# Seven gate products placed last in the input part with a PSUM bank of their own, put-off closing sums, and low-rank weights by head pair

## The chip, the cores and the metric

The kernel runs on one core of a Trainium2 chip. The metric is the device time of one execution in microseconds; the lower the better. TensorE is PE in the rows (its weight loads are PEld), VectorE DVE, ScalarE ACT, GpSimd POOL and SyncE SP.

## The reference

One hybrid encoder layer is computed for a prompt of 1024 rows and a sample of 256 rows, in float32 with 1024 channels. Cut to the part that the change touches:

```python
h = rmsnorm(x, norm_mix) * (1.0 + sc1) + sh1          # sh, sc, g: silu(c) @ w_ada + b_ada
p = h @ w_in                                          # 672 | 1792 | 2048 columns
p_mla, p_rwkv, p_gate = ...
xs = pf + mu_shift * (centred_shift(pf) - pf)         # pf = p_rwkv; r, k, v, wd, ad, gd are parts of xs
g = sigmoid(gd) @ w_gate_up
kk = k * k_k / norm over the head;  tw = tanh(wd)
for d in range(2):                                    # two directions
    wlog = -softplus(-(w0[d] + tw @ w_decay_up[d])) - 0.5
    a = sigmoid(a0[d] + ad @ w_iclr_up[d])
    k_d = k * (1.0 + (a - 1.0) * k_a)
    y = y + wkv_scan(...);  bonus_k = bonus_k + k_d
out = (group_norm(y) * lnx_w + lnx_b + sum(r * bonus_k * r_k) * v) * g
gm, gr = split(sigmoid(p_gate))
x = x + g1 * ((gm * o_mla + gr * o_rwkv) @ w_out)     # then a SwiGLU FFN
```

## The kernel before, in words

Both sequences stand side by side as T = 1280 columns, with channels on the 128 partitions. A product of 1024 by 128 channels takes the columns in three chunks of 512, 512 and 256 (`CH`). To keep float32 precision each operand is split into a high and a low part, and `gemm` (line 67) does three matmuls for each of 8 row tiles and each chunk: 72 in all, into three PSUM banks at a time. `split_w` loads the weights (`wraw`, line 51), casts the high part on ScalarE (`whi`, line 53) and subtracts on GpSimd or VectorE (`wlo`, line 55).

After the normalised input `hh`, `hl` is there, the input part has 27 such products. First come two for the low-rank inputs. Then four head pairs follow (`pt`), each with products for k, r and v; each product is evacuated to `pp` (line 299, two buffers) and shifted on VectorE (lines 302 to 305). Per pair and direction four small low-rank products (line 352) go through two `aux` banks to tanh on ScalarE (lines 384 and 391), and VectorE makes `kd` and `ka` from them; results are spilled to DRAM. At the pair's end come `bk`, a head sum (line 363) and the bonus. Then `phase_mla_in` has six products with two norms and the rotary keys `kpe`, and after them the first seven of the sixteen gate products, whose tanh (line 457) is spilled. The other nine are computed much later. The pieces of the w_ada product that are needed later (lines 162, 170 to 182) are called by a hook inside the products: one piece after row tiles 1, 4 and 7, each with a load of 512 KB into one of two `araw` buffers; after four pieces the result is transposed by eight small products, and it takes an `araw` buffer for this (`am4`).

The order of the instructions on each engine is laid out when the kernel is built: a planner with a cost model gives the engine the ready instruction that was emitted first, so what is emitted later fills places that are free in the planner's own timeline. Buffers and banks are waited for one by one. On the chip every engine follows its list in order, and so do the DMA queues of SP, ACT and POOL. PSUM has eight banks: five for products (`mm`), two `aux`, one for the w_ada pieces. Attention follows; its tiles use the memory of `hh`, `hl` and of the weight buffers.

## Time and profile before

| | |
|---|---|
| time, 3 runs | 2739.36, 2742.91 (median), 2749.71 us |
| profiled execution | 2739.23 us, span 2737.5 us |
| TensorE busy | 2528.6 us (92%), 16458 matmuls |
| VectorE busy | 1464.8 us (54%) |
| ScalarE busy | 987.5 us (36%) |
| GpSimd busy | 844.4 us (31%) |
| DMA | 273.39 MB, mean 100 GB/s |

The busy time is that of one profiled execution, and the shares are of its span. In rows of a timeline the first number is the start in us from the span's start, the second the length; "x3" means three instructions merged into one row, and the bracket says how long the engine stood idle before and what ended that. In the rows by stretch, the numbers behind the length are the busy us of PE, PEld, DVE, ACT and POOL with the count of instructions, then the granted TensorE clock as a share of full speed, the share of DMA time and GB/s.

### The profile page before, as it was taken

The page shows a single profiled execution, that of the slowest core. Times are in us where ns is not written, and L with a number is a line of the kernel's source. Part 1 is how long each engine was busy: PE and PEld are TensorE (multiplying, and loading weights), DVE is VectorE, ACT ScalarE, POOL GpSimd, SP SyncE. Part 2 cuts the span into 40 slices and gives each one's busy share as a digit, 9 for nine tenths or more (in the row PEclk, how much of TensorE's full clock was granted, in tenths as well). Part 3 has the DMA queues.
Part 4 walks back from the last instruction along what each step waited for, and adds up shares of the span by engine and source line. Part 5 has one row for each costly group of instructions (what it writes and reads, how often), then busy time and mean ns, then how long its engine had stood idle before and what let it go on. Part 6 is the DMA issues. An engine that isn't in the chain of part 4 may idle for free.

```text
span 2737.5 us, 41260 instructions
## 1 busy us (share of the span) xinstructions
PE 2528.6 (92%) x16458; PEld 2139.5 (78%) x16458; DVE 1464.8 (54%) x2436; ACT 987.5 (36%) x1853; POOL 844.4 (31%) x820
## 2 busy tenths in 40 slices
PE   5998879999998889899989988899999999999997
PEld 3776558888987778888877767778888888888886
DVE  6664553237777688988986557362222222222228
ACT  4432223236776645556553233241110111101114
POOL 1112122121015654455544466342111111111123
PEclk9999889999999888899978899999999999999998
DMA  7645432210003432533445755221111111111113
GB/s 292 213 179 194 166 123 67 77 48 16 18 15 86 147 102 80 164 104 117 147 128 175 233 173 152 94 70 62 39 39 32 38 39 39 39 39 39 39 39 131
DMA packets 175279, 273.39 MB, mean 100 GB/s; under 512 B 14752, under 2 KB 103792, under 8 KB 175088
## 3 DMA queue, kind: packets, MB, share of 16 engines
q1 hardware_dynamic: 169328, 244.55, 27.9%
q0 software_dynamic: 5760, 26.22, 2.4%
q8 instruction: 129, 2.11, 0.3%
q14 instruction: 62, 0.51, 0.1%
HBM read 202.51 MB, written 68.20 MB: 99 GB/s over the span
## 4 chain that ended last, share of the span: by engine, by line
PE 71%; DVE 19%; DMA 3%; issue 3%; ACT 2%; POOL 2%; SPq 1%; POOLq 0%; DVEq 0%; ACTq 0%
PE mm L67 46%; PE fp L1004 7%; DVE W L832 3%; PE s L592 3%; DVE xt L830 3%; PE o L626 2%; PE proj L525 2%; PE t L613 2%; PE py L877 1%; DVE lt L772 1%; DVE tt L834 1%; PE ada_ps L170 1%; PE lora L352 1%; PE pA L785 1%; PE hsum L363 1%
## 5 line engine op out<-in xcount | busy, mean ns | idle before, releaser
L55 POOL TENSOR_TENSOR wlo<-wraw,whi 128x512 fp32r<-128x512 f32 (+2 forms) x226 | 404.0, 1789 | 1165.3 <-ACT whi L53 1129.1
L53 ACT CAST whi<-wraw 128x1024 fp32r<-128x1024 f32 (+2 forms) x241 | 193.9, 806 | 954.8 <-issue 466.8
L67 PE MATMUL mm<-h2h,whi 128*128 128x512 f32 (+1 forms) x1056 | 280.2, 358 | 1.5 <-ACT whi L53 1.5
L67 PE MATMUL mm<-h2h,wlo 128*128 128x512 f32 (+1 forms) x1056 | 279.8, 358 | 1.3 <-POOL wlo L55 1.3
L67 PE MATMUL mm<-h2l,whi 128*128 128x512 f32 (+1 forms) x1056 | 279.4, 357 | 0.0
L67 PE MATMUL mm<-g,whi 128*128 128x512 f32 (+1 forms) x1056 | 240.1, 359 | 6.2 <-DVE ft L1209 5.6
L1004 PE MATMUL fp<-x,whi 128*128 128x256 f32 (+1 forms) x912 | 220.5, 334 | 12.6 <-DVE gt L1139 4.1
L67 PEld LDWEIGHTS mm<-g,whi 128*128 128x128 f32 x1056 | 177.4, 189 | 38.0 <-issue 5.7
L67 PEld LDWEIGHTS mm<-h2h,whi 128*128 128x128 f32 x1056 | 177.5, 189 | 33.2 <-ACT whi L53 1.8
L67 PEld LDWEIGHTS mm<-h2h,wlo 128*128 128x128 f32 x1056 | 177.5, 189 | 32.9 <-POOL wlo L55 2.2
L67 PEld LDWEIGHTS mm<-h2l,whi 128*128 128x128 f32 x1056 | 177.4, 188 | 31.5 <-issue 0.5
L67 PE MATMUL mm<-hh,whi 128*128 128x512 f32 (+1 forms) x648 | 188.1, 368 | 11.0 <-ACT pp L299 6.3
L67 PE MATMUL mm<-hl,whi 128*128 128x512 f32 (+1 forms) x648 | 185.8, 364 | 7.0 <-DVE hl L244 7.0
L1221 DVE SCALAR_TENSOR_TENSOR x<-mm,g2h,x 128x512 f32<-128x512 f32 (+1 forms) x144 | 86.9, 656 | 195.9 <-PE mm L67 195.6
L1004 PEld LDWEIGHTS fp<-x,whi 128*128 128x128 f32 x912 | 165.9, 215 | 25.4 <-ACT whi L53 5.3
L67 PE MATMUL mm<-hh,wlo 128*128 128x512 f32 (+1 forms) x648 | 184.4, 364 | 0.0
L1209 DVE SCALAR_TENSOR_TENSOR ft<-ft,mm 128x512 f32<-128x512 f32 (+1 forms) x66 | 36.1, 593 | 223.5 <-ACT ft L1208 223.4
L1004 PE MATMUL fp<-x,wlo 128*128 128x256 f32 (+1 forms) x456 | 151.4, 333 | 0.4 <-POOL wlo L55 0.4
L1210 DVE TENSOR_TENSOR ft<-ft,mm 128x512 f32<-128x512 f32 (+1 forms) x66 | 36.0, 593 | 215.9 <-PE mm L67 215.9
L67 PEld LDWEIGHTS mm<-hh,whi 128*128 128x128 f32 x648 | 116.3, 193 | 38.5 <-ACT pp L299 8.0
L67 PEld LDWEIGHTS mm<-hl,whi 128*128 128x128 f32 x648 | 116.6, 192 | 30.6 <-DVE hl L244 8.2
L67 PE MATMUL mm<-g,wlo 128*128 128x512 f32 (+1 forms) x528 | 135.6, 358 | 1.2 <-POOL wlo L55 1.2
(310 smaller groups left out, 5071.9 us busy)
## 6 DMA issues: line engine op xcount, KB each, us to landing
wraw<-in_w_ffn_in_dram SPq DMA_DIRECT2D x56, 512.0 KB, 3.6
araw<-in_w_ada_dram SPq DMA_DIRECT2D x48, 512.0 KB, 3.5
wraw<-in_w_in_dram SPq DMA_DIRECT2D x27, 512.0 KB, 3.5
wraw<-in_w_in_dram SPq DMA_DIRECT2D x54, 256.0 KB, 3.8
wraw<-in_w_ffn_out_dram SPq DMA_DIRECT2D x26, 512.0 KB, 3.5
x<-scr_h SPq DMA_DIRECT2D x20, 512.0 KB, 6.9
gt<-scr_gate SPq DMA_DIRECT2D x32, 256.0 KB, 2.7
wraw<-in_w_out_dram SPq DMA_DIRECT2D x32, 256.0 KB, 2.6
```

The lines of the kernel that those rows point to most:

```text
L53: nc.scalar.copy(hi, raw)
L55: (eng or nc.gpsimd).tensor_tensor(lo, raw, hi, ALU.subtract)
L67: nc.tensor.matmul(p[:, :n], lhsT=ww[:, k, :], rhs=aa[:, k, c0:c0 + n], start=(k == 0 and i == 0), stop=(k == kt - 1 and i == 2))
L525: nc.tensor.matmul(p[:, :n], lhsT=ww[:, k, :], rhs=aa[:, k, c0:c0 + n], start=(k == 0 and i == 0), stop=(k == kt - 1 and i == 2))
L592: nc.tensor.matmul(s[:, o:o + w], lhsT=a[:, tt * P:(tt + 1) * P], rhs=b[:, c0 + o:c0 + o + w], start=(m == 0), stop=(m == 2))
L613: nc.tensor.transpose(t[:, j, :], prs[i][:, kk * P:(kk + 1) * P], g.ident)
L626: nc.tensor.matmul(o, lhsT=vs[h // 4][:, c0 // P + kk, h % 4, :], rhs=pts[j][m][kk // 4][:, kk % 4, :], start=(kk == 0 and m == 0), stop=( ...
L830: nc.vector.tensor_tensor(tv, W[:, h:, j:j + 1].broadcast_to([P, n, j]), X[:, j:j + 1, 0:j].broadcast_to([P, n, j]), ALU.mult)
L832: nc.vector.tensor_tensor(W[:, h:, 0:j], W[:, h:, 0:j], tv, ALU.add)
L1004: g.nc.tensor.matmul(p[:, c:c + n], lhsT=ww[:, k % 4, :], rhs=aa[:, k, :n], start=(k == 0 and i == 0), stop=(k == kt - 1 and i == 2))
L1209: nc.vector.scalar_tensor_tensor(t[:, :n], t[:, :n], 1.0, u[:, :n], ALU.add, ALU.mult)
L1221: nc.vector.scalar_tensor_tensor(x1[:, dt, c0:c0 + n], p[:, :n], g.g2h[:, dt, c0 // TP:c0 // TP + 1], x1[:, dt, c0:c0 + n], ALU.mult, ALU.add)
```

## The change

The seven gates leave `phase_mla_in`. A new function `gates` is emitted after it. It takes each gate's weights in two halves from a pool of its own (one raw buffer, two high and two low halves), and goes chunk by chunk through one PSUM bank of its own (`gps`); the products' banks go from five to four. Each chunk's tanh is stored by ScalarE's DMA queue. The hook becomes a class that can also put off work: the closing product of w_ada comes three calls later and has its own `am4` buffer, and the bonus of pairs 0 to 2 comes three calls into the next pair's first product. The hook's w_ada loads go from SP's to ScalarE's queue. The low-rank weights are loaded, cast and split per head pair (one load of 128x640) instead of once at the start, into single buffers. `phase_mla_in` has five `m5` buffers instead of six, and `kpe` holds its low part in the lower half of one tile.

```diff
@@ -159,7 +159,7 @@
 def ada_load(g, pool, cb, q, bufs):
     raw = pool.tile([P, 4, 256], F32, tag="araw", name="araw", bufs=bufs)
-    g.nc.sync.dma_start(out=raw, in_=g.io["w_ada"][cb, q])
+    (g.nc.scalar if bufs == AW else g.nc.sync).dma_start(out=raw, in_=g.io["w_ada"][cb, q])
...
-    def piece(k):
-        if k % 3 != 1 or not todo:
+class Hook:
...
+    def later(self, n, fn):
+        self.off.append([n, fn])
+    def fetch(self, i):
+        if i < len(self.todo) and self.todo[i] not in self.raw:
+            self.raw[self.todo[i]] = ada_load(self.g, self.pool, *self.todo[i], AW)
+    def __call__(self, k, ada=True):
+        for o in self.off:
+            o[0] -= 1
+        due = [o for o in self.off if o[0] <= 0]
+        self.off = [o for o in self.off if o[0] > 0]
+        for _, fn in due:
+            fn()
+        if not ada or k % 3 != 1 or not self.todo:
             return
-        cb, q = todo.pop(0)
+        g = self.g
+        self.fetch(0)
+        cb, q = self.todo[0]
         if q == 0:
-            box.append(g.ap.tile([P, 512], F32, name="ada_ps"))
-        ada_piece(g, box[0], q, ada_load(g, pool, cb, q, AW))
+            self.ps = g.ap.tile([P, 512], F32, name="ada_ps")
+        ada_piece(g, self.ps, q, self.raw.pop((cb, q)))
+        self.todo.pop(0)
         if q == 3:
-            ada_close(g, cb, box.pop(), pool.tile([P, 512], F32, tag="araw", name="am4", bufs=AW))
-    return piece
+            m = self.pool.tile([P, 512], F32, tag="am4", name="am4", bufs=1)
+            g.nc.scalar.copy(m, self.ps)
+            self.later(3, lambda: ada_close(g, cb, m))
...
-        rest = ada_hook(g, rw, range(4, 12))
+        hook = Hook(g, rw, range(4, 12))
         def in_tile(ct):
             w = split_w(g, io["w_in"][ct], KT, nc.vector if ct % 3 in WV else None, rbufs=1)
-            return gemm(g, w, (hh, hl), KT, hook=ct > 1 and rest)
+            return gemm(g, w, (hh, hl), KT, hook=lambda k: hook(k, ct > 1))
-        wlh = rw.tile([P, 5, 512], F32R, tag="wlh", name="wlh")
...
-            wl = t5("wl")[:, 0:512]
-            blk, e = (i // 2, i % 2) if i < 4 else (2, 0)
-            if i < 4:
-                for r in HV:
-                    nc.sync.dma_start(out=wl[r], in_=io["w_lora"][HV[e], blk, :])
-            else:
-                nc.sync.dma_start(out=wl, in_=io["w_lora"][:, blk, :])
-            nc.scalar.copy(wlh[:, i, :], wl)
...
-            r = HV[e] if i < 4 else slice(0, P)
-            nc.vector.tensor_tensor(wll[r, i, :], wl[r], wlh[r, i, :], ALU.subtract)
+        def low_rank(pt):
+            raw = t5("wl")[:, 0:640].rearrange("p (i n) -> p i n", n=P)
+            nc.sync.dma_start(out=raw, in_=io["w_lora"][pt])
+            h, l = (rw.tile([P, 5, P], F32R, tag=t, name=t) for t in ("wlh", "wll"))
+            nc.scalar.copy(h, raw)
+            nc.vector.tensor_tensor(l, raw, h, ALU.subtract)
+            for e in range(2):
+                nc.vector.memset(l[HV[1 - e], 2 * e:2 * e + 2, :].bitcast(F32), 0.0)
+            return h, l
...
-        def lora(pt, *terms):
+        def lora(*terms):
             ps = []
-            cs = slice(pt * P, (pt + 1) * P)
...
-        def stacked(pt, d, e):
-            return lora(pt, (wlh[:, 2 * d + e], st[e]), (wll[:, 2 * d + e], st[e]))
+        def stacked(w, d, e):
+            return lora(*((x[:, 2 * e + d, :], st[e]) for x in w))
...
         for pt in range(4):
+            wl = low_rank(pt)
             k = shifted(in_tile(2 + 3 * pt), 2 + 3 * pt)
...
-            bo = t5("bo")
-            headsum(bk, lambda p, s: nc.vector.tensor_tensor(bo[:, s], p, v[:, s], ALU.mult))
-            ps = lora(pt, (wlh[:, 4], sgh), (wlh[:, 4], sgl), (wll[:, 4], sgh))
...
+            def bonus(pt=pt, bk=bk, v=v, wl=wl):
+                bo = t5("bo")
+                headsum(bk, lambda p, s: nc.vector.tensor_tensor(bo[:, s], p, v[:, s], ALU.mult))
+                ps = lora((wl[0][:, 4], sgh), (wl[0][:, 4], sgl), (wl[1][:, 4], sgh))
...
+            if pt < 3:
+                hook.later(3, bonus)
+            else:
+                bonus()
+def gates(g, hh, hl):
+    nc, io = g.nc, g.io
+    for j in range(NB):
+        ws = [split_w(g, io["w_in"][20 + j][:, k0:k0 + 4, :], 4, pool=g.gp, tag="gw", rbufs=1) for k0 in (0, 4)]
+        for c0, n in CH:
+            p = g.gps.tile([P, 512], F32, name="gps")
+            for k in range(KT):
+                wh, wl = ws[k // 4]
+                for i, (ww, aa) in enumerate(((wh, hh), (wh, hl), (wl, hh))):
+                    nc.tensor.matmul(p[:, :n], lhsT=ww[:, k % 4, :], rhs=aa[:, k, c0:c0 + n],
+                                     start=(k == 0 and i == 0), stop=(k == KT - 1 and i == 2))
+            t = g.gp.tile([P, 512], F32, tag="gate", name="gate", bufs=1)
+            nc.scalar.activation(t[:, :n], p[:, :n], AF.Tanh, scale=0.5)
+            nc.scalar.dma_start(out=g.scr["gate"][j, :, c0:c0 + n], in_=t[:, :n])
...
                 ps = gemm(g, split_w(g, io["w_in"][ct0 + j], KT, rbufs=1), (hh, hl), KT)
-                pv.append(ml.tile([P, T], F32, tag="m5", name="pv", bufs=6))
+                pv.append(ml.tile([P, T], F32, tag="m5", name="pv", bufs=5))
...
         nc.vector.tensor_tensor(kr[H, :], kr[H, :], ksw[H, :], ALU.add)
-        nc.scalar.copy(kpe[0][H, :], kr[H, :])
-        nc.vector.tensor_tensor(kpe[1][H, :], kr[H, :], kpe[0][H, :], ALU.subtract)
-        for j in range(NB):
-            ps = gemm(g, split_w(g, io["w_in"][20 + j], KT, rbufs=1), (hh, hl), KT)
-            t = ml.tile([P, T], F32, tag="m5", name="gate", bufs=6)
-            for p, (c0, n) in zip(ps, CH):
-                nc.scalar.activation(t[:, c0:c0 + n], p[:, :n], AF.Tanh, scale=0.5)
-            nc.sync.dma_start(out=g.scr["gate"][j], in_=t)
+        nc.scalar.copy(kpe[H, :], kr[H, :])
+        nc.vector.tensor_tensor(kpe[0:64, :], kr[H, :], kpe[H, :], ALU.subtract)
...
-            for j in range(2):
-                (nc.gpsimd if i else nc.vector).tensor_copy(kb[i][j][64:128, :], kpe[j][64:128, :])
+            (nc.gpsimd if i else nc.vector).tensor_copy(kb[i][0][64:128, :], kpe[64:128, :])
+            (nc.scalar.copy if i else nc.vector.tensor_copy)(kb[i][1][64:128, :], kpe[0:64, :])
...
-                    psum(g, c3, mm=5, aux=2, ap=1)
+                    psum(g, c3, mm=4, aux=2, ap=1, gps=1)
                     phase_start(g, hh, hl)
+                    g.gp = c3.enter_context(tc.tile_pool(name="gp", bufs=1, reuse_waits="tile"))
                     phase_rwkv_in(g, hh, hl)
...
-                    kpe = [lat.tile([P, T], F32R, name=f"kpe{i}") for i in range(2)]
+                    kpe = lat.tile([P, T], F32R, name="kpe")
...
                     phase_mla_in(g, hh, hl, qc, kc, kpe)
+                    gates(g, hh, hl)
                     mod_rest(g)
...
-    wl = np.concatenate([np.concatenate([g("w_decay_up")[0].transpose(1, 0, 2), g("w_iclr_up")[0].transpose(1, 0, 2)], 0), g("w_gate_up")[0][:, None, :]], 1)
-    o["w_lora"] = np.ascontiguousarray(wl)
+    wd, wa = g("w_decay_up")[0], g("w_iclr_up")[0]
+    wl = np.stack([np.concatenate([x, x], 0) for x in (wd[0], wd[1], wa[0], wa[1])] + [g("w_gate_up")[0]], 1)
+    o["w_lora"] = np.ascontiguousarray(wl.reshape(P, 5, 4, P).transpose(2, 0, 1, 3))
```

## Rows read from the trace of the kernel before

**Rows 1.** the page's chain that ended last: shares of the span by engine

```profile
PE 71%; DVE 19%; DMA 3%; issue 3%; ACT 2%; POOL 2%; SPq 1%; POOLq 0%; DVEq 0%; ACTq 0%
```

**Rows 2.** busy time by stretch: start:end, length, engines' busy us, granted clock, DMA share, GB/s

```profile
57.07:577.05 519.98, 477.01 (x2493) 375.42 (x2491) 243.35 (x277) 162.14 (x241) 96.53 (x127) 0.95 0.40 145
57.07:237.00 179.93, 178.05 (x960) 135.49 (x958) 108.77 (x115) 68.61 (x99) 31.94 (x58) 0.99 0.58 209
237.00:252.00 15.00, 6.34 (x39) 4.63 (x38) 13.14 (x14) 2.42 (x5) 4.39 (x12) 0.66 0.76 279
310.00:331.00 21.00, 8.66 (x56) 6.20 (x55) 17.13 (x19) 2.90 (x6) 5.50 (x13) 0.59 0.53 201
384.50:410.00 25.50, 7.10 (x22) 3.73 (x21) 20.74 (x25) 1.94 (x5) 5.07 (x5) 0.67 0.29 118
410.00:490.50 80.50, 79.20 (x415) 66.53 (x416) 25.02 (x48) 30.51 (x44) 14.86 (x7) 1.00 0.19 64
490.50:577.00 86.50, 86.50 (x456) 73.93 (x454) 10.02 (x9) 15.93 (x27) 12.96 (x5) 1.00 0.19 71
```

**Rows 3.** TensorE's waits, 57 to 577 us: us in total, times, longest

```profile
PE hsum L363 <- DVE bk L405: 16.7, 1, 16.7
PE ada_ps L170 <- DMA araw<-in_w_ada_dram: 14.7, 4, 4.8
PE mm L67 <- ACT pp L299: 6.3, 2, 4.3
```

**Rows 4.** timeline of TensorE, 251 to 332 us: start us, us, what, idle before

```profile
251.88 0.28 PE L67 MATMUL mm<-hl,whi 128*128 128x256 f32 x1
252.00 0.28 PE L67 MATMUL mm<-hh,wlo 128*128 128x256 f32 x1
...
325.31 0.58 PE L67 MATMUL mm<-hh,whi 128*128 128x256 f32 x1 [4.26 <-ACT pp L299]
325.69 0.42 PE L67 MATMUL mm<-hl,whi 128*128 128x256 f32 x1
325.91 0.41 PE L67 MATMUL mm<-hh,wlo 128*128 128x256 f32 x1
```

**Rows 5.** timeline of VectorE and of POOL at 387 us

```profile
387.74 3.15 DVE L465 TENSOR_SCALAR g2h<-modT 128x16 f32<-128x16 f32 x1
...
387.95 2.89 POOL L402 TENSOR_TENSOR bk<-kd 128x1280 f32<-128x1280 f32 x1
```

**Rows 6.** timeline of ACT, 521 to 537 us

```profile
521.70 1.35 ACT L457 ACTIVATE gate<-mm 128x512 f32<-128x512 f32 x3
...
535.65 1.35 ACT L457 ACTIVATE gate<-mm 128x512 f32<-128x512 f32 x3
```

**Rows 7.** timeline of TensorE at the last gate's end

```profile
578.17 0.73 PE L525 MATMUL proj<-kc,whi 128*128 128x512 f32 x2 [1.10 <-ACT gate L457]
```

**Rows 8.** POOL's timeline at 596 us, and the page's DMA issues

```profile
596.35 1.29 POOL L542 TENSOR_TENSOR q<-qf,q 128x512 fp32r<-128x512 f32 x1 [3.87 <-PE proj L525]
...
wraw<-in_w_in_dram SPq DMA_DIRECT2D x54, 256.0 KB, 3.8
```

**Rows 9.** SyncE's waits, 0 to 577 us, and its timeline at 494 us

```profile
SPq L162 <- PE ada_ps L170: 60.5, 23, 8.5
...
494.58 0.33 SPq L458 DMA_DIRECT2D scr_gate<-gate  x1
```

**Rows 10.** timeline of ACT at 490 us

```profile
490.65 1.28 ACT L457 ACT_TABLE_LOAD   x1
```

**Rows 11.** timelines of ACT and of TensorE, 345 to 363 us

```profile
345.97 0.47 ACT L415 ACTIVATE wg<-lora,vec 128x256 f32<-128x256 f32 x1 [1.61 <-DVE bo L413]
...
358.77 0.39 PE L352 MATMUL lora<-st,wlh 128*128 128x512 f32 x1
362.76 0.40 PE L352 MATMUL lora<-st,wlh 128*128 128x512 f32 x1
```

**Rows 12.** timeline of VectorE at 500 us

```profile
500.41 1.49 DVE L452 TENSOR_TENSOR kpe<-ktab,kpe 64x1280 fp32r<-64x1280 f32 x1 [1.32 <-ACT kpe L451]
```

More of the change, by code (lines that the diff above doesn't have):

```diff
@@ L183, in ada_close, with __init__ @@
                             g.vec[:, a + 4 * cb:a + 4 * cb + 4].unsqueeze(2).broadcast_to([P, 4, 2]), ALU.add)
-def ada_hook(g, pool, cbs):
-    todo = [(cb, q) for cb in cbs for q in range(4)]
-    box = []
-    def piece(k):
-        if k % 3 != 1 or not todo:
+class Hook:
+    def __init__(self, g, pool, cbs):
+        self.g, self.pool = g, pool
+        self.todo = [(cb, q) for cb in cbs for q in range(4)]
+        self.off, self.ps, self.raw = [], None, {}
+    def later(self, n, fn):
[11 more added lines that the diff above has]
+        if not ada or k % 3 != 1 or not self.todo:
             return
-        cb, q = todo.pop(0)
+        g = self.g
+        self.fetch(0)
+        cb, q = self.todo[0]
         if q == 0:
-            box.append(g.ap.tile([P, 512], F32, name="ada_ps"))
-        ada_piece(g, box[0], q, ada_load(g, pool, cb, q, AW))
+            self.ps = g.ap.tile([P, 512], F32, name="ada_ps")
+        ada_piece(g, self.ps, q, self.raw.pop((cb, q)))
+        self.todo.pop(0)
         if q == 3:
-            ada_close(g, cb, box.pop(), pool.tile([P, 512], F32, tag="araw", name="am4", bufs=AW))
-    return piece
+            m = self.pool.tile([P, 512], F32, tag="am4", name="am4", bufs=1)
+            g.nc.scalar.copy(m, self.ps)
+            self.later(3, lambda: ada_close(g, cb, m))
 def ada_first(g, pool, cb, raws):
@@ L206, in ada_first @@
         ada_piece(g, ps, q, raws[q])
-    ada_close(g, cb, ps, pool.tile([P, 512], F32, tag="am", name="am", bufs=1))
+    m = pool.tile([P, 512], F32, tag="am", name="am", bufs=1)
+    g.nc.scalar.copy(m, ps)
+    ada_close(g, cb, m)
 def gain(g, out, sc, norm, w=KT, j=0):
@@ L380, in phase_rwkv_in @@
             for d in range(2):
-                ps = stacked(pt, d, 0)
+                ps = stacked(wl, d, 0)
                 s2 = t5("s2")
@@ L438, in phase_mla_in @@
         H = slice(64, 128)
-        tab = [ml.tile([P, T], F32, tag="m5", name="ktab", bufs=6) for _ in range(2)]
+        tab = [ml.tile([P, T], F32, tag="m5", name="ktab", bufs=5) for _ in range(2)]
         for i in range(2):
@@ L442, in phase_mla_in @@
             nc.sync.dma_start(out=tab[i][H, TP:], in_=io["ktab"][:, i, :TS])
-        ksw = ml.tile([P, T], F32, tag="m5", name="ksw", bufs=6)
+        ksw = ml.tile([P, T], F32, tag="m5", name="ksw", bufs=5)
         kr = tab[0]
```

29 lines of the change are left out of this document (12 added, 17 removed).

## The prediction

> **What bounds the kernel now.** I read the chain of waits first, then the busy time by stretch, then who waited for whom. The chain that ended last is TensorE for 71% and VectorE for 19% [rows 1]. So what counts is where TensorE stands still. Everything that the change touches lies between the first input product and the start of attention, 57.07 to 577.05 us of the trace. TensorE is busy there for 477.01 of 519.98 us and idle for 42.97 [rows 2]. The idle time is in three stretches: 15.00 - 6.34 = 8.66 us (237 to 252), 21.00 - 8.66 = 12.34 (310 to 331), 25.50 - 7.10 = 18.40 (384.5 to 410); together 39.4. Between them, and in the first 180 us (178.05 of 179.93), TensorE is full. The seven gates run last, from about 480 to 577, in a stretch without a gap (86.50 of 86.50) [rows 2].
>
> What makes the gaps? The list of waits names the sum of line 363 waiting for VectorE (16.7 us), DMA of w_ada (14.7) and the evacuation `pp` (6.3) [rows 3]. The w_ada waits are not the cause: behind them the next product stands for `pp`, which waits for VectorE, and in the second gap it starts only at 325.31, with `pp` as its releaser [rows 4]. In each gap VectorE is the busy one (13.14 of 15.00, 17.13 of 21.00, 20.74 of 25.50) [rows 2]. It has two shifts (`xs`) and the `kd`/`ka` work in a row, and TensorE has by then run ahead as far as its five product banks allow: one whole product and two chunks of the next. Work that needs neither those banks nor VectorE could run there.
>
> A second loss lies behind each gap: products of 256 columns follow each other at 0.21 us (325.69 to 325.91), against 0.12 us at full rate (251.88 to 252.00) [rows 4]; the mean granted clock of the three stretches is 0.66, 0.59 and 0.67 [rows 2], a mix of the 1.2 and 2.4 GHz levels after standing still. At 0.09 us each, 18 such matmuls in the first gap cost 1.7 us and 24 in the second 2.3; with the w_ada pieces and head sums that run slow beside them, some 3 us by the same ratio, I put it at 7 us.
>
> **The change, part by part.** *The gates as filler.* One gate costs 13.95 us (its evacuations begin at 521.70 and 535.65 [rows 6]), so seven are 97.7 us of TensorE. Emitted last, they have the lowest claim and go where nothing else is ready when the order is laid out. The whole gain possible is what they can cover: 42.97 + 7 = 50 us.
>
> A gate now runs chunk by chunk through one bank: 5.58 us for 512 columns (13.95 x 512/1280) twice and 2.79 for 256. Before the next chunk the bank has to be read out. The price lies between the read-out alone, 0.45 us on average (1.35 for three [rows 6]), and the 1.10 us that a product once waited for such a read-out [rows 7]; I take 0.85 after a wide chunk and 0.6 after the narrow one, 2.3 us a gate. Alone in a gap a gate thus uses 13.95/16.25 = 86% of it. Of the 39.4 us, 34 are filled and 5.5 stay; I add 3 for the first gate weights of a gap coming late.
>
> *The gates that are left.* If 34 us go into the gaps and some 20 more into places where four product banks instead of five make a product wait, or where the laid-out order shows a gap that the chip doesn't have, 97.7 - 54 = 44 us, three gates, stay behind the last input product. There nothing covers the bank wait (2.3 us). Nor the weights: half of a gate's weights can be fetched only when POOL has read the half before from the single raw buffer, so DMA 3.8 us for 256 KB and POOL 1.29 us for 128x512 [rows 8] stand in a row, and a cast between them: 5.1 us without the cast, against the 2.8 us that 12 wide matmuls run. I take 2.4 us of stall a gate (between 0 and 2.8). 4.7 us a gate, three gates: 14 us. Against it, `vs[0]` of attention lies where the input weights lay, so some of the 60 value products (256 columns, so 0.12 us each [rows 4], 7 us) can slip in: 4 us back.
>
> *Four product banks, `m5` with five buffers.* TensorE runs ahead one chunk of the next product, not two, 5.6 us less per gap, and has it still to do afterwards. While gates last this only changes the order, so 0; without them it is 3 gaps x 5.6 = 17 us.
>
> *Gate weights on POOL among the rwkv work.* VectorE and POOL get in each other's way: a 128x16 operation took 3.15 us beside POOL's `bk` of 2.89 [rows 5]. Fourteen subtractions of 1.29 us [rows 8] are 18 us at most if all strike a VectorE burst; perhaps half do, 9 us of VectorE. TensorE has gates to run meanwhile: 0, and 9 to 18 if it has none. The Trainium skill ("SBUF — State Buffer", Who interferes with whom) says that a VectorE operation in a two-port mode, or one with two SBUF inputs against a GpSimd operation that reads SBUF, and the GpSimd operation exclude each other for a whole instruction, and whichever starts first holds the ports. The trace agrees in the 3.15 beside 2.89. By that rule nearly all of VectorE's work in the gaps would pay, so the 18 and not the 9: the sum of the forecast stays, and the half case below would win 6 us and not 15.
>
> *w_ada loads on ACT's queue.* SP waited 60.5 us in 23 cases for a piece to free its buffer [rows 9], without harm. On ACT the same wait holds up what is queued behind: `pp` and the low-rank activations, which TensorE and VectorE wait for. ACT is busy 162.14 of 519.98 us [rows 2], so 32 issues of 0.33 us [rows 9], and 21 more for gate chunks that SP stored in 7, 17 us, fit. Bounds: 0, and 8.5 us (the longest wait) in each of three gaps; I take 2 us. On SP, 14 gate-weight loads that wait for POOL to free the raw buffer now stand ahead of product weights; those are fetched a product ahead and no wait for them is among TensorE's [rows 3]: 0, at most 5 us (DMA and POOL as above) a gap. SP no longer waits for w_ada, a gain of 0 while TensorE is full. The separate `am4` buffer and the closing product three calls later take away a wait of which the list of TensorE shows nothing here [rows 3]: 0.
>
> *Table loads.* A gate tanh between square roots means new table loads of 1.28 us [rows 10]. Eight more are 10 us on an engine that is two thirds idle: 0.
>
> *Low-rank weights per pair.* Nine loads at 75 to 85 us become four of 320 KB; the elements cast and subtracted stay the same, and leave a stretch in which TensorE is full anyway [rows 2]: 0. New is that a pair's weights can be rewritten only after the put-off bonus of the pair before. Before, the first low-rank product of pair 3 (358.77) came about 12 us after the last bonus activation (345.97 + 0.47) [rows 11]; a cast and a subtraction of 640 columns, at rates like the 1.29 us for 512 on POOL, are under 3. So 0, or up to 3 us in each of three pairs.
>
> *Rotary part.* One `kpe` tile instead of two, and two of the four `kb` copies on POOL go to ACT: 0, as attention's first products need only `kc` and a free bank [rows 7].
>
> **Sum.** 50 - 5.5 - 3 - 14 + 4 - 2 = 29.5, say 30 us. Against the profiled execution (2739.23, span 2737.5) that is 2709; that execution stands 3.7 us under the median of 2742.91, so on the scale of the median 2713.
>
> **Rivals.** *Packed:* the gates are all used among input products, nothing is left at the end: 50 - 8 with small losses, 2700 down to 2692. For it: between the gaps the laid-out order leaves TensorE next to no idle time, so where it has something ready it is used. Against: from 410 to 490 only 80.50 - 79.20 = 1.3 us is idle [rows 2], so after the third gap gates have no place.
>
> *Half:* the gates go early. In 57 to 237 TensorE has no idle time, so gates put there only push everything back; the third gap (18.4 us, and 17 us by fewer banks spread over the gaps) stays as it was, and the VectorE lock counts. For it: between two low-rank products TensorE does nearly 4 us of other work (358.77 to 362.76) though ACT needs only about 0.7 for a read-out [rows 11], so the planned order rates TensorE faster against ACT than it is, and sees more gaps than there are. 30 - 18 + 3 = about 15: 2728.
>
> *Slower:* the gates are gone before the last input product, and the end that they covered comes into the open: from the last product at about 490 to `kpe` at 500.41 + 1.49 = 501.90 [rows 12], 11.4 us, and then no gap has been filled on the chip but the 17 us of shorter run-ahead is paid in part (I take 8), with 8 us won in the first gap. It decides from the point where all 97.7 us of gates stand before the second gap. 2743 + 11 + 8 - 8 = 2754.
>
> *Not as it says:* the order leaves the gates at the end (weights or bank too late to fit in). Then seven run one bank each, 7 x 4.7 = 33 us more, 2776.
>
> **Chances.** Forecast 0.50, its own range 2702 to 2726; packed 0.15; half 0.18; slower 0.10; not as it says 0.07. About 0.5%, 13.7 us, can be told from no change: the forecast and packed and half of the half case are faster, 0.74; the other half and the slower case (2754 is within) 0.17; 0.09 slower. Range for 8 in 10: 2688, the packed case with its error, to 2743, which leaves out the last two.
>
> **What would show it.** In the trace after: TensorE's idle from 57 us to attention's first product below 25 us; `gps` matmuls inside VectorE's bursts; clock 0.95 or more there; two to four gates behind the last `mm` product of the input part, with 0.6 to 1.1 us before each chunk and a wait for `wlo` or DMA at its second half; attention beginning near 547. Wrong if gates finish before 300 us and a gap of over 12 us remains, if ACT's queue stands in w_ada issues, or if attention and what follows change in length by more than 5 us.

## The result and the profile after

The changed kernel takes 2700.86 us (median of 4 runs, 2696.32 to 2702.14) against 2745.85 us before (2739.36 to 2749.71) beside it: ratio 0.9836, interval 0.9811 to 0.986. That is 45 us less, where 30 were forecast. The time lies inside the predicted range of 2688 to 2743, and 1 us under the forecast's own range of 2702 to 2726. The profiled execution took 2696.32 us (span 2694.6), before 2739.23 (2737.5); both are the fastest of their runs, so their stages can be compared. The difference of the spans, 42.9 us, is made up of these parts:

| stretch, from the last product of one stage to that of the next | before | after | difference |
|---|---|---|---|
| input part (57 us to the last input or gate product) | 519.8 | 491.9 | -27.9 |
| attention (to its last `o` product) | 320.0 | 320.4 | +0.4 |
| scan with its fill (to the last fill product, `fp<-x`) | 658.5 | 645.5 | -13.0 |
| joining of the branches (to the last `fp`) | 204.1 | 207.8 | +3.7 |
| feed-forward (to its last product of `g`) | 956.8 | 951.2 | -5.6 |
| end | 21.3 | 20.8 | -0.5 |

So the input part gave what was forecast, and some 15 us came from stages of which the change edits no line. "Fill" is what `phase_fill` emits for the places that the scan leaves free on TensorE: the other nine gates and the output projection of attention.

The chain of waits after (shares of the span by engine), which answers to [rows 1]: TensorE has lost three points, VectorE has gained two.

```profile
PE 68%; DVE 21%; DMA 3%; issue 3%; ACT 2%; POOL 2%; SPq 0%; DVEq 0%; POOLq 0%; ACTq 0%
```

Busy time by stretch after, with the columns of [rows 2]; the last four rows are the scan, the fill behind its last product (`py`), the joining and the feed-forward.

```profile
57.00:549.00 492.00, 471.22 (x2504) 372.78 (x2503) 252.30 (x278) 167.06 (x249) 99.08 (x134) 0.99 0.42 155
57.00:231.00 174.00, 171.64 (x924) 134.16 (x923) 105.86 (x106) 67.69 (x97) 34.86 (x58) 0.99 0.57 213
231.00:250.00 19.00, 14.58 (x96) 11.24 (x95) 17.68 (x18) 4.38 (x10) 7.96 (x15) 0.94 0.61 210
322.00:331.00 9.00, 8.08 (x52) 6.28 (x53) 6.66 (x11) 2.95 (x6) 3.63 (x12) 1.00 0.99 362
388.00:420.00 32.00, 26.86 (x119) 20.07 (x118) 20.60 (x24) 5.84 (x12) 8.76 (x8) 0.95 0.35 133
420.00:498.00 78.00, 76.15 (x414) 64.96 (x413) 20.51 (x43) 26.67 (x38) 10.29 (x6) 1.00 0.16 52
498.00:549.00 51.00, 44.98 (x221) 35.21 (x221) 12.98 (x12) 14.67 (x22) 5.76 (x4) 1.00 0.18 59
...
869.30:1500.70 631.40, 558.42 (x6039) 506.59 (x6037) 508.31 (x1008) 340.45 (x746) 322.59 (x414) 0.87 0.44 134
1500.70:1514.80 14.10, 14.10 (x87) 12.56 (x85) 4.91 (x9) 3.10 (x6) 5.14 (x4) 1.00 0.91 294
1514.80:1722.60 207.80, 184.06 (x901) 148.40 (x899) 125.00 (x177) 63.43 (x115) 123.34 (x92) 0.98 0.52 163
1722.60:2673.80 951.20, 934.43 (x4788) 791.47 (x4787) 304.91 (x447) 177.56 (x274) 210.21 (x92) 0.99 0.15 48
```

TensorE's idle time in the input part fell from 42.97 to 492.00 - 471.22 = 20.78 us, and its busy time fell by 477.01 - 471.22 = 5.8 us at a granted clock of 0.99 instead of 0.95, though 12 key products of attention (`proj`, 2.3 us) now stand in this part. Together that is 28 us. The three gaps were idle for 39.4 us before, at clocks of 0.66, 0.59 and 0.67. They are now idle for 19.00 - 14.58 = 4.4, 0.9 and 5.1 us, at 0.94, 1.00 and 0.95.

Busy time of the gate matmuls (`gps`) alone, by stretch (PE, PEld, ACT with counts, then clock, DMA share, GB/s): most stand in and around the three gaps, where VectorE works in a row, and the rest behind the last input product. In the three gap stretches (231 to 250, 322 to 331 and 388 to 420) the same view gives 8.1, 3.1 and 22.5 us of them, some 34 in all.

```profile
160.00:180.00 20.00, 5.05 (x19) 3.41 (x19) 0.00 (x0) 1.00 0.71 253
220.00:250.00 30.00, 10.45 (x53) 8.31 (x53) 1.62 (x3) 0.96 0.64 230
300.00:330.00 30.00, 15.15 (x72) 11.80 (x72) 1.19 (x2) 1.00 0.56 212
380.00:430.00 50.00, 30.85 (x142) 23.40 (x142) 2.76 (x5) 0.97 0.43 160
500.00:550.00 50.00, 40.84 (x201) 31.94 (x199) 4.74 (x9) 1.00 0.18 60
```

TensorE's waits after, 57 to 549 us (us in total, times, longest): neither the sum of line 363 nor w_ada, first and second in [rows 3], is among the first four now.

```profile
PE gps L453 <- ACT gate L456: 9.4, 13, 1.9
PE mm L67 <- ACT pp L320: 3.9, 2, 3.6
PE gps L453 <- POOL wlo L55: 2.6, 3, 1.2
PE gps L453 <- ACT whi L53: 2.5, 2, 2.2
```

The timeline of TensorE behind the last input product (start, length, what, idle before and releaser): four places where it waits, and for what.

```profile
518.43 0.50 PE L453 MATMUL gps<-hh,wlo 128*128 128x512 f32 x1 [0.80 <-POOL wlo L55]
...
521.68 0.50 PE L453 MATMUL gps<-hh,whi 128*128 128x512 f32 x1 [0.69 <-ACT gate L456]
...
528.10 0.39 PE L453 MATMUL gps<-hh,whi 128*128 128x256 f32 x1 [0.69 <-ACT gate L456]
...
531.70 0.50 PE L453 MATMUL gps<-hh,whi 128*128 128x512 f32 x1 [0.47 <-ACT gate L456]
```

The timeline of ACT beside it has the read-outs of the last two, 0.60 us for 512 columns and 0.38 for 256:

```profile
527.45 0.60 ACT L456 ACTIVATE gate<-gps 128x512 f32<-128x512 f32 x1 [5.82 <-PE gps L453]
...
531.26 0.38 ACT L456 ACTIVATE gate<-gps 128x256 f32<-128x256 f32 x1 [0.89 <-PE gps L453]
```

Then the stretches of the scan before, and of the fill behind its last product: 174 matmuls stand there in 38.3 us, where after there are 87 in 14.1. The scan itself is longer after (631.4 against 620.2), with 88 more matmuls in it.

```profile
896.80:1517.00 620.20, 555.00 (x5951) 501.00 (x5950) 502.07 (x1000) 336.37 (x742) 317.68 (x410) 0.85 0.43 130
1517.00:1555.30 38.30, 34.21 (x174) 28.94 (x173) 21.32 (x37) 7.46 (x13) 16.98 (x13) 0.90 0.79 258
```

In the feed-forward the wait of a norm's sum for VectorE makes most of the difference; before, and then after (us, times, longest):

```profile
PE nb_ps L83 <- DVE acc L1171: 6.3, 2, 5.1
```

```profile
PE nb_ps L83 <- DVE acc L1205: 1.2, 1, 1.2
```

### The profile page after: what moved, and what is told of

It is laid out like the page before. It is cut to its first block, busy times and chain, and to the rows that moved or that the text cites. A ratio compares the mean times of both kernels' runs of the same rounds, so it can differ in the third digit from the quotient of the medians.

```text
span 2694.6 us, 41304 instructions
## 1 busy us (share of the span) xinstructions
PE 2502.5 (93%) x16458; PEld 2124.3 (79%) x16458; DVE 1479.8 (55%) x2439; ACT 994.8 (37%) x1863; POOL 844.2 (31%) x825
## 4 chain that ended last, share of the span: by engine, by line
PE 68%; DVE 21%; DMA 3%; issue 3%; ACT 2%; POOL 2%; SPq 0%; DVEq 0%; POOLq 0%; ACTq 0%
PE mm L67 43%; PE fp L1038 6%; DVE W L866 3%; DVE xt L864 3%; PE s L626 3%; PE o L660 2%; PE proj L559 2%; PE gps L453 2%; PE t L647 2%; DVE lt L806 2%; DVE tt L868 1%; PE lora L369 1%; PE ada_ps L170 1%; PE py L911 1%; PE pA L819 1%
## 5 line engine op out<-in xcount | busy, mean ns | idle before, releaser
L55 POOL TENSOR_TENSOR wlo<-wraw,whi 128x512 fp32r<-128x512 f32 (+3 forms) x233 | 406.3, 1746 | 1190.8 <-ACT whi L53 1155.9
L53 ACT CAST whi<-wraw 128x512 fp32r<-128x512 f32 (+2 forms) x248 | 195.1, 789 | 921.3 <-issue 468.2
L1038 PE MATMUL fp<-x,whi 128*128 128x256 f32 (+1 forms) x912 | 214.3, 329 | 8.6 <-ACT x L1020 3.7
L67 PE MATMUL mm<-hh,whi 128*128 128x512 f32 (+1 forms) x480 | 148.1, 366 | 6.8 <-ACT pp L320 3.9
L67 PE MATMUL mm<-hl,whi 128*128 128x512 f32 (+1 forms) x480 | 147.4, 364 | 7.5 <-DVE hl L265 7.5
L67 PE MATMUL mm<-hh,wlo 128*128 128x512 f32 (+1 forms) x480 | 146.2, 364 | 0.0
L864 DVE TENSOR_TENSOR xt<-W,X 128x126 f32<-128x126 f32 (+22 forms) x310 | 124.3, 401 | 9.4
L866 DVE TENSOR_TENSOR W<-W,xt 128x126 f32<-128x126 f32 (+22 forms) x310 | 123.6, 399 | 9.7
```

The costliest lines, as they stand in the source:

```text
L53: nc.scalar.copy(hi, raw)
L55: (eng or nc.gpsimd).tensor_tensor(lo, raw, hi, ALU.subtract)
L67: nc.tensor.matmul(p[:, :n], lhsT=ww[:, k, :], rhs=aa[:, k, c0:c0 + n], start=(k == 0 and i == 0), stop=(k == kt - 1 and i == 2))
L864: nc.vector.tensor_tensor(tv, W[:, h:, j:j + 1].broadcast_to([P, n, j]), X[:, j:j + 1, 0:j].broadcast_to([P, n, j]), ALU.mult)
L866: nc.vector.tensor_tensor(W[:, h:, 0:j], W[:, h:, 0:j], tv, ALU.add)
L1038: g.nc.tensor.matmul(p[:, c:c + n], lhsT=ww[:, k % 4, :], rhs=aa[:, k, :n], start=(k == 0 and i == 0), stop=(k == kt - 1 and i == 2))
```

## The experiments

The theories: the gates in the gaps make the 28 us of the input part; and for the 15 us behind it, theory A, that the order of the later part came out another way when the whole program was laid out anew, against theory B, that the input part leaves something behind (the clock, DMA traffic, memory) that makes the later part faster. The stages of all profiled executions in one table (us; "behind" is the number of fill matmuls that stand behind the scan's last product in the order as laid out; "norm" the wait of the feed-forward's norm sum):

| run | input part ends (idle) | attention | behind | scan and fill | norm | feed-forward | median time |
|---|---|---|---|---|---|---|---|
| before | 576.8 (43.0) | 320.0 | 171 | 658.5 | 6.3 | 956.8 | 2743.8 to 2747.5 |
| e1 | 577.3 (43.0) | 320.2 | 171 | 661.6 | 6.3 | 957.4 | 2742.3 |
| after | 548.9 (20.8) | 320.4 | 84 | 645.5 | 1.2 | 951.2 | 2700.9 |
| e2 | 549.2 (21.3) | 322.1 | 84 | 644.3 | 1.2 | 951.1 | 2705.8 |
| e3 | 579.7 (46.7) | 318.8 | 108 | 649.1 | 5.8 | 957.8 | 2725.8 |
| e4 | 497.5 (56.2) | 338.2 | 84 | 653.7 | 3.3 | 955.8 | 2673.5 |
| e5 | 574.6 (42.3) | 319.2 | 84 | 654.1 | 3.3 | 957.3 | 2732.2 |
| e6 | 548.4 (16.6) | 322.3 | 153 | 665.9 | 5.8 | 958.4 | 2719.1 |
| e7 | 549.9 (20.6) | 322.4 | 84 | 650.6 | 1.2 | 951.6 | 2704.4 |
| e8 | 542.0 (15.6) | 327.5 | 84 | 646.6 | 5.8 | 958.4 | 2705.5 |
| e9 | 551.6 (20.8) | 322.4 | 174 | 680.4 | 3.3 | 956.3 | 2734.2 |
| e10 | 550.2 (20.5) | 320.0 | 84 | 653.7 | 3.3 | 955.4 | 2720.5 |
| e11 | 586.9 (52.2) | 319.1 | 84 | 648.5 | 3.3 | 956.2 | 2741.0 |
| e12 | 548.4 (16.7) | 322.5 | 84 | 650.2 | 5.8 | 958.0 | 2708.4 |

Executions of one kernel differ by up to some 19 us (e2: 2696 to 2715), and a profile is one of them: those of e3, e5, e6, e7 and e9 lie 2 to 10 us above their kernel's median, those of e2 and e10 10 us below it. So a single length of the scan's stage is good to several us only, and the medians weigh more.

**The two kernels again (e1, e2), without an edit.**

> The kernel before, a second profile. Asked: in the first pair of profiles 28 us of the 43 lie before attention, and some 15 after it, 13 of them between the last attention value product and the last fill product (658.7 us before, 645.7 after). Theory A (the order laid out for the later part is another, and its place on the clock with it): this stretch is 657 to 661 us again, the input part ends at 577 +- 1. Theory B (chance from execution to execution): it comes out anywhere between 640 and 665.

> The changed kernel once more, with a second profile. Input part: last gate product ends at 549 +- 1 in any case. Theory A: the stretch from the last attention value product to the last fill product is 644 to 648 us again and the ratio 0.982 to 0.986. Theory B: the stretch moves by over 5 us, and the ratio by over 0.003.

e1 took 2742.27 us in one run, e2 2705.77 (ratio 0.9847, 0.981 to 0.9883). Every stage repeats within 3.1 us. The 13 us of the scan's stage and the 5.6 of the feed-forward thus belong to the program and are no chance of one execution. Both profiles of the changed kernel are of executions of 2696 us, though.

**The gates back at the end (e3)**, with five product banks, all other edits kept:

```diff
         nc.vector.tensor_tensor(kpe[0:64, :], kr[H, :], kpe[H, :], ALU.subtract)
+        for j in range(NB):
+            ps = gemm(g, split_w(g, io["w_in"][20 + j], KT, rbufs=1), (hh, hl), KT)
...
-                    psum(g, c3, mm=4, aux=2, ap=1, gps=1)
+                    psum(g, c3, mm=5, aux=2, ap=1)
...
-                    gates(g, hh, hl)
```

> All of the change but the gates: they stand at the end of the latent part again, three chunks at a time, with five product banks; the hook, w_ada on ScalarE's queue, the put-off sums and the low-rank weights per pair stay as changed. Theory 1 (the gates filling VectorE's bursts are the gain): the three gaps are back, TensorE idle 38 to 48 us in the input part, which ends at 570 to 582, and the time is 2725 to 2750. Theory 2 (the other edits are the gain): gaps of VectorE stay small, end at 545 to 555, time 2695 to 2710. The later part is open: with theory A it is laid out anew and may be 10 us to either side.

2725.75 us, ratio 0.9913 (0.9885 to 0.9941). The input part is back where it was, and a little worse than before:

```profile
57.00:579.70 522.70, 475.96 (x2493) 378.79 (x2494) 249.72 (x281) 162.03 (x242) 98.01 (x127) 0.94 0.39 145
```

Idle is 522.70 - 475.96 = 46.7 us at a clock of 0.94. So the gates as filler make the whole gain of the input part, and the other edits (w_ada on ACT's queue, the put-off closing and bonus, low-rank weights by pair, `kpe`) together lose about 3 us there. The time is nevertheless some 20 us below that of before: this kernel shows the later gain with the gates back at the end, with 108 fill matmuls behind the scan.

**No gates at all (e4).**

```diff
-                    gates(g, hh, hl)
+                    t = g.gp.tile([P, 512], F32, tag="gate", name="gate", bufs=1)
+                    nc.vector.memset(t, 0.0)
...
+                            nc.scalar.dma_start(out=g.scr["gate"][j, :, c0:c0 + n], in_=t[:, :n])
```

> Leaves the seven gates out (zeros are stored in their place, so the result is not the reference's). Theory 1: four of the seven cost nothing where they stand, so only the 51 us of the last three go: products end at 495 to 505 as before, with gaps of TensorE of 45 to 65 us (four banks run less far ahead than five), and attention starts at 500 to 512. Rival (gates delay the products that they stand among): the input part ends 75 us or more earlier, at 475 or below.

The kernel leaves the seven gates out and takes 2673.5 us in one run. Its input part:

```profile
57.00:497.50 440.50, 384.32 (x1986) 297.62 (x1986) 232.10 (x269) 138.71 (x206) 89.70 (x120) 0.91 0.46 164
```

Without gates TensorE is idle for 440.50 - 384.32 = 56.2 us. Seven gates of 13.95 us (97.7) lengthen this part by 548.9 - 497.5 = 51.4 us, so about 46 us of them run for nothing. Of that, 56.2 - 20.8 = 35.4 us is idle time filled. The other 11 us come with the clock, 0.99 instead of 0.91: TensorE's busy time grows by only 86.9 us. The gates left at the end cover something too. Without them attention takes 338.2 us instead of 320.4: TensorE waits 3.4 us for `kc` before its first products and 8.4 us for `v`, where after there is only a wait of 4.2 us for `v`. By the end of attention the seven gates have cost 869.3 - 835.7 = 33.6 us.

**One edit alone on the kernel before: w_ada on ACT's queue (e5)**, taken because the order laid out for it has 84 fill matmuls behind the scan.

```diff
-    g.nc.sync.dma_start(out=raw, in_=g.io["w_ada"][cb, q])
+    (g.nc.scalar if bufs == AW else g.nc.sync).dma_start(out=raw, in_=g.io["w_ada"][cb, q])
```

> The kernel before with one edit: the hook's w_ada loads are issued from ScalarE's queue. Its order has 84 fill products after the scan's last product, as the changed kernel has, where the kernel before has 171. Theory A (the 15 us behind attention come from another laid-out order of fill and scan, which any small edit can bring): input part 574 to 580 us as before, scan and fill 643 to 650 us instead of 658 to 662, time 8 to 18 us under before (ratio 0.993 to 0.997). Theory B (the later gain needs the gates in their new place, or is chance): scan and fill 657 to 663, ratio 0.998 to 1.002.

2732.23 us, ratio 0.9934 (0.9908 to 0.9959). The input part is 2 us shorter, the scan's stage 654.1 us: 4 to 8 less than before, but above the 643 to 650 of theory A. The median is 15 us down against 2747.48 of before in the same comparison, and the profiled execution lies 4 us above it. So some of the later gain comes with an edit that leaves the gates where they were, though not all of it.

**w_ada back on SP's queue in the changed kernel (e6).**

```diff
-    (g.nc.scalar if bufs == AW else g.nc.sync).dma_start(out=raw, in_=g.io["w_ada"][cb, q])
+    g.nc.sync.dma_start(out=raw, in_=g.io["w_ada"][cb, q])
```

> The changed kernel with the hook's w_ada loads on SP's queue as before. Its order has 153 fill products after the scan's last product instead of 84. The gates' order among the products is the same to the count (202 matmuls of 504 behind the last product). Theory 1 with A: input part ends at 547 to 553, so the queue is worth nothing there, but scan and fill take 654 to 661 us, time 8 to 15 us over the changed kernel (2708 to 2716). Rival (the queue matters: SP held product weights up): input part 555 us or later. Rival B: scan and fill 643 to 648, time as the changed kernel.

2719.12 us, ratio 0.9896 (0.9868 to 0.9924). The input part ends at 548.4 instead of 548.9, but the equal ends hide something. In this execution the clock was 0.50 in 57 to 62 us, where it was 0.72 in the other, and the first gap comes 1.1 us later. In that gap the read-out of a narrow gate chunk is early on ACT, and the next chunk follows at once; in the changed kernel it stands behind three `pp` copies that wait for VectorE. The rows of e6, then of the changed kernel:

```profile
243.74 0.39 ACT L456 ACTIVATE gate<-gps 128x256 f32<-128x256 f32 x1 [2.04 <-PE ada_ps L170]
```

```profile
245.69 0.59 ACT L320 COPY pp<-mm 128x512 f32<-128x512 f32 x1 [4.98 <-DVE xs L326]
...
247.39 0.43 ACT L456 ACTIVATE gate<-gps 128x256 f32<-128x256 f32 x1
```

From 231 to 250 us TensorE is idle for 1.4 us with SP and 4.4 with ACT, in the whole input part for 16.6 and 20.8. Being 1.1 us late in the first gap and 0.5 us early at the end, e6 gains about 1.6 us. The changed kernel repeats this gap in e2 (4.4 us idle); of e6 there is one profile.

Behind the scan 153 fill matmuls stand in e6, its stage takes 665.9 us, somewhat more than theory A's 654 to 661, and the feed-forward takes 958.4. So what is lost against the changed kernel is lost there.

**The bonus not put off (e7).**

```diff
-            if pt < 3:
-                hook.later(3, bonus)
-            else:
-                bonus()
+            bonus()
```

> The changed kernel with the bonus of all four pairs emitted where it was before; the w_ada closing products stay put off. 84 fill products after the scan, as in the changed kernel. Prediction's step (putting off is worth nothing, 0 to 3 us a pair): input part ends at 546 to 552 and the time is that of the changed kernel within 5 us. Rival (putting off keeps TensorE from waiting at a pair's end): gaps at the pairs' ends return, the input part ends at 556 or later.

2704.43 us, ratio 0.9843 (0.9823 to 0.9864): no difference from the changed kernel that can be told. Input part 549.9.

**The last three gates through three banks (e8)**, two of them `aux`; the bonus as in e7.

```diff
-            p = g.gps.tile([P, 512], F32, name="gps")
+            p = g.gps.tile([P, 512], F32, name="gps") if j < 4 or c0 == 512 else g.aux.tile([P, 512], F32, tag="mm", name="gps")
```

> As the last kernel (bonus in its old place), but gates 4 to 6 put their first and last chunk into the two aux banks, so that a chunk need not wait for the read-out of the chunk before. Prediction's step (the single bank costs 0.6 to 0.85 us a chunk where nothing else is left): the bank waits of the last three gates, about 4.3 us of 6 idle in 498 to 549, go; input part ends 3 to 5 us earlier than with one bank. Rival (weights from the single raw buffer are the limit, the prediction's 2.4 us a gate): the waits move to wlo and whi, and the end moves by under 2 us. 84 fill products after the scan.

2705.48 us, ratio 0.985 (0.9826 to 0.9875). The busy time by stretch shows the end of the input part with hardly a wait, 43.08 busy of 44.00 us:

```profile
498.00:542.00 44.00, 43.08 (x222) 35.97 (x220) 12.74 (x12) 14.43 (x22) 5.22 (x4) 1.00 0.19 62
```

The part ends 7 to 8 us earlier, where 3 to 5 were expected. The waits of TensorE from 542 to 600 us, and the row of ACT at its end, show where that went first:

```profile
PE proj L556 <- ACT gate L453: 4.9, 1, 4.9
```

```profile
546.71 0.38 ACT L453 ACTIVATE gate<-gps 128x256 f32<-128x256 f32 x1 [4.45 <-DMA scr_gate<-gate]
```

A product of attention waits for the read-out of the last gate chunk. That read-out in turn waits 4.45 us until the store before it has landed, because there is one `gate` buffer; a second one was not tried. Attention takes 327.5 us instead of 322.4 in e7. The feed-forward takes 7 us more as well, with the norm's wait at 5.8. A gain in one stage, given back in the next.

**The fill in another order, the input part untouched (e9, e10).** `LAG` is the number of the fill's nine gates that run two chunks at a time: 9, here 7 and 8.

```diff
-QB, MR, FR, LAG, KS, FP, RB, WB = 3, 4, 4, 9, 4, 2, 2, 2
+QB, MR, FR, LAG, KS, FP, RB, WB = 3, 4, 4, 7, 4, 2, 2, 2
```

> The changed kernel with one number of the fill altered that runs beside the scan (its gate products in pairs of chunks: 7 instead of 9), the input part untouched. In the order that results 174 fill products stand behind the scan's last product, about as before the change (171), where the changed kernel has 84. Theory A (the 13 us that scan and fill lost, and the 5 behind them, hang on how the order of that later part comes out): input part ends at 548 to 550 as in the changed kernel, scan and fill take 655 to 664 us instead of 645, time 2711 to 2722, so more than half of what the changed kernel gains behind attention is gone. Rival B (they hang on what the input part leaves behind: the clock, DMA traffic, where the tiles lie): scan and fill stay at 643 to 648, time 2698 to 2706.

```diff
-QB, MR, FR, LAG, KS, FP, RB, WB = 3, 4, 4, 9, 4, 2, 2, 2
+QB, MR, FR, LAG, KS, FP, RB, WB = 3, 4, 4, 8, 4, 2, 2, 2
```

> The same edit with 8 instead of 9; in this order 84 fill products stand behind the scan, as in the changed kernel. It tells whether the edit itself costs something: theory A: input part ends at 548 to 550, scan and fill 643 to 648, time 2698 to 2706. If the edit costs by itself (more weights fetched for single chunks): 2706 or more, and the run with 7 is to be read against this one.

e9: 2734.2 us (10 runs), ratio 0.9957 (0.9942 to 0.9972). e10: 2720.54, ratio 0.9902 (0.9875 to 0.9929). The scan and the fill behind it, of e9 and of e10:

```profile
874.00:1514.40 640.40, 567.29 (x5948) 515.80 (x5947) 513.73 (x999) 342.73 (x753) 327.27 (x418) 0.83 0.43 128
1514.40:1554.40 40.00, 34.12 (x177) 28.54 (x176) 20.78 (x37) 7.96 (x14) 17.08 (x13) 0.93 0.81 258
```

```profile
870.20:1506.40 636.20, 567.29 (x6039) 511.67 (x6037) 511.03 (x1008) 342.25 (x751) 328.82 (x418) 0.85 0.45 133
1506.40:1523.90 17.50, 14.56 (x90) 12.48 (x86) 4.12 (x8) 3.38 (x6) 5.06 (x4) 1.00 0.84 254
```

The input parts end within 2.7 us of the changed kernel's, yet most of its gain is gone in e9. That is against theory B. It is also more than theory A gave: the scan's stage takes 680.4 us, not 655 to 664. Between e9 and e10, 40.0 - 17.5 = 22.5 us lie behind the scan, as 38.3 - 14.1 = 24.2 did between before and after; the medians lie 13.7 us apart. But e10 misses what theory A gave it (2698 to 2706): with 84 matmuls behind, it is still 15 to 20 us slower than the changed kernel by the medians (2705.77 and 2700.86), so the edit of the fill, or another part of the order it brings, costs something by itself, and e9 has to be read against e10. In its profile, 13.6 us longer than that of the changed kernel, the scan takes 636.2 us instead of 631.4, the stretch behind it 3.4 us more, and the feed-forward 4.2. So the count behind the scan is one part of the order's worth and not all of it.

**The kernel before with four product banks (e11).**

```diff
-                    psum(g, c3, mm=5, aux=2, ap=1)
+                    psum(g, c3, mm=4, aux=2, ap=1)
```

> The kernel before with four product banks instead of five and nothing else. The prediction's term: without gates as filler each of the three gaps grows by 5.6 us, so the input part takes 519.8 + 17 = 537 us. Rival: the order laid out for four banks, or work still to be done behind the gap, takes most of it back: 520 to 526. By theory A of the later part (84 fill products behind the scan in this order) scan and fill take 644 to 655 us instead of 658 to 662.

2741.04 us, ratio 0.999 (0.9977 to 1.0003). Its input part, scan and fill behind the scan:

```profile
57.00:586.90 529.90, 477.68 (x2493) 376.79 (x2492) 247.39 (x275) 162.22 (x240) 96.03 (x127) 0.94 0.40 142
906.00:1540.40 634.40, 565.82 (x6039) 511.44 (x6037) 512.66 (x1008) 340.55 (x746) 323.55 (x414) 0.87 0.44 133
1540.40:1554.50 14.10, 14.10 (x88) 12.56 (x85) 4.66 (x9) 3.12 (x6) 5.15 (x4) 1.00 0.92 277
```

The fifth bank is worth 529.9 - 519.8 = 10 us in the input part where no gates fill the gaps; both expectations of it missed, 17 and 0 to 6. The time hides that, as the scan's stage is 10 us shorter, with 14.1 us behind the scan as in the changed kernel. The input part grew, and the later gain came all the same, without the gates. This speaks against theory B too; but four banks are an edit of the input part, and e9 is the cleaner case.

**Gate weights in quarters through two raw buffers (e12)**, the bonus as in e7.

```diff
-        ws = [split_w(g, io["w_in"][20 + j][:, k0:k0 + 4, :], 4, pool=g.gp, tag="gw", rbufs=1) for k0 in (0, 4)]
+        ws = [split_w(g, io["w_in"][20 + j][:, k0:k0 + 2, :], 2, pool=g.gp, tag="gw", rbufs=2, bufs=4) for k0 in (0, 2, 4, 6)]
...
-                wh, wl = ws[k // 4]
+                wh, wl = ws[k // 2]
```

> The changed kernel with the gate weights in quarters through two raw buffers instead of halves through one, and the bonus not put off (which alone moved nothing). 84 fill products behind the scan. Theory: weights hold TensorE only some 2 us in the 51 us behind the last input product and 2 to 3 in the gaps, so the input part ends at 545 to 550 and the time is 2698 to 2706. Rival (gates fill the gaps only to 84% because the second half of the weights comes late): the input part ends at 538 to 544, the time is 2690 to 2697.

2708.39 us, ratio 0.9859 (0.9842 to 0.9877). Idle falls by 4 us (16.7), the input part by 1.5 us (548.4 against 549.9 in e7), and the time not at all; it lies 2 us above the expected 2698 to 2706. The waits for the gates' weights were 5.3 us in e7, and shortening them won no more than that. No version that computes the gates is faster than the changed kernel.

## Why the prediction was right where it was, and where it was not

*What bounds the input part, and the gates as filler: right.* 28 us were won where 30 were forecast; e3 takes them all back, e4 shows about 46 us of gates running for nothing. Some 34 us of gate matmuls stand in the three gaps, as in the sum. Of the signs named, these came: idle 20.8 us (under 25), `gps` matmuls in VectorE's bursts, clock 0.99, 202 of the 504 gate matmuls, 2.8 gates, behind the last input product in TensorE's order, 0.69 us of wait before a chunk, attention from 549 (547 forecast). One of the signs of being wrong came too: what follows changed by more than 5 us.

*The slow clock behind the gaps: 5.8 us came back, or about 8 without the 12 key products, 7 forecast.* (The two starts of [rows 4] lie 0.22 us apart, not 0.21; that moves the 7 by less than 1.)

*The losses were mis-sized, and the errors cancelled.* The sum left 50 - 29.5 = 20.5 us of loss; measured are 20.8 us of idle. In the gaps 5.5 + 3 = 8.5 were forecast and 4.4 + 0.9 + 5.1 = 10.4 stayed. The gates left at the end were to cost 14 us and cost 51.00 - 44.98 = 6.0: about 2 us a gate, not 4.7. The bank waits came to 4.3 us in seven cases (mostly 0.69 behind a wide chunk and 0.47 behind a narrow one, for the 0.85 and 0.6 of the sum), but the weights, put at 2.4 us a gate, made TensorE wait 1.7 us in all, and the load takes 3.1 us now (median of 68), 3.8 before [rows 8]. Over all gates the bank cost 9.4 us in 13 cases, for 21 chunks. The other way, 57.00 to 231.00 and 420.00 to 498.00 are idle for 2.4 and 1.9 us, which had no term. The 4 us of value products that were to slip in did not: the first `pv` starts at 550.4, behind the gates; 12 of the 18 `proj` products of keys came ahead instead (2.3 us), and brought nothing: attention then waits 4.2 us for `v`, against 1.5 before, and keeps its length.

*ACT's queue: about the 2 us taken, in the changed kernel.* e6 shows some 1.6 us, but not by the forecast way: no wait of a load is seen to hold `pp` up there, a gate's read-out stands later in ACT's order. In the kernel before, the same edit made the part 2 us shorter (e5), so the price is not one of the queue alone. The put-off bonus (e7): 1 us or nothing. Table loads: 13 in the input part, 11 before, so two more and not eight. The low-rank weights: no wait for them is among those of TensorE. With all the small edits and no gates in the gaps (e3) the input part is 3 us longer than before; the bound for the weights alone was 3 us in each of three pairs.

*Four product banks.* The prediction put them at 17 us without filler and 0 with it. e11 measured 10 for the first.

*VectorE beside GpSimd.* 9 us of VectorE were put on the gates' subtractions, 18 at most. With the gates at the end (e3) VectorE is busy for 249.72 us, among the products 252.30: 2.6 us more. But the totals hide what happened to single operations. Those that lie beside a gate's own subtraction on GpSimd are together 5.7 us longer than the shortest of their kind in these kernels. The shifts (`xs`, `pp`) take 85.3 us instead of 72.2, with the subtractions and other GpSimd work beside them, and small ones like `nb_dg` take 4.1 instead of 8.5. So VectorE's bursts did grow, by 13 us, and TensorE had gates to run meanwhile, as the prediction said. The Trainium skill ("SBUF — State Buffer", Who interferes with whom) has a VectorE operation with two SBUF inputs, or in a two-port mode, and a GpSimd operation that reads SBUF exclude each other for a whole instruction; by that rule the prediction preferred 18 to 9, and the runs show 5.7 for the subtractions. The row behind it fits the exclusion: the 128x16 operation of 3.15 us takes 0.16 in the changed kernel, where no GpSimd work runs beside it. It does not fit that whichever starts first holds the ports, as VectorE's is recorded first (387.74 against 387.95) and was held to the end of the other.

*The step that failed: "attention and what follows" unchanged.* It was an unspoken term of 0 in the sum, and by the prediction's own sign (5 us) it was wrong: it measured -15 us, of which scan and fill -13.0, feed-forward -5.6, joining +3.7. Attention itself kept its length (320.4). The program is laid out as one, so an edit in the input part also gave the fill a new order: 84 matmuls behind the scan's last product instead of 171, which leaves 14.1 us instead of 38.3 behind it, and the scan with the other fill in it is 11 us longer. Two edits of the old kernel that leave the gates alone bring much of the same: e5's median is 15 us below that of before, and e11 pays 10 us in the input part and takes the time of before. Two edits that leave the input part of the new kernel nearly as it is take it away: e9 is 33 us slower than the changed kernel's 2700.86 (28 by the 2705.77 of e2), and e10, the like edit with 84 matmuls behind, 20 (15). e6 is 18 (13) slower. The intervals of e6 and e10 still touch that of e2, that of e9 does not. So this part comes with the layout of the later stages, and the gates are not needed for it. Without it the time would be near 2718, in the middle of the forecast's own range.

*The rivals.* That the time came out at the 2700 of the packed case is chance: packed had no gates at the end, and 2.8 were there. Half: the third gap took 22.5 us of gates and its idle time fell from 18.4 to 5.1, so the gates were not gone early; the slower case falls with it. Not as it says: 302 of the 504 gate matmuls came ahead of the last input product.

What stays open: why the scan itself takes 620 us in one layout and 631 to 640 in others with equal or more fill inside (before and e9 have the same number behind), and why the norm's wait in the feed-forward is 1.2, 3.3 or about 6 us. The runs show that these go with the program; no run isolated what in the order makes them.

## What to carry to other kernels

Independent work with a bank and weights of its own, emitted last, can fill the places where TensorE waits for VectorE: 97.7 us of it cost 51 by the end of this part, and 34 by the end of attention. What is left over at the end costs little beside its bank waits. Where the whole program is laid out at once, an edit at the front also shuffles what comes later; that was worth 13 us here and some 30 in a variant, as much as the edit itself. So compare stage by stage, and judge the edit by its own stage and by a control that gives the later part another order.

## What was not expected of the hardware

Where ScalarE is free at once, a single bank costs little more than its read-out: TensorE stood still for 0.69 us behind a read-out of 0.60, and for 0.47 behind one of 0.38, so 0.09 us more in both cases. The prediction had put 0.85 and 0.6 from other rows. The other of the 13 bank waits lie between 0.26 and 1.85 us. And the third gap, which keeps 5.1 us of idle time out of 32 in waits of at most 2.2 us, has a granted clock of 0.95; before, idle for 18.4 us out of 25.5 with one wait of 16.7, it had 0.67.
